# A hybrid decoder layer: the attention loop written in program order, with queries packed on GpSimd

## The chip, the core and the metric

The kernel runs on one core of a Trainium2 chip. The metric is the device time of one launch in microseconds. The core has five engines, each with an instruction stream of its own: TensorE (PE, matmuls and transposes, with its weight loads PEld), VectorE (DVE), ScalarE (ACT), GpSimd (POOL) and SyncE (SP). SP and ACT also issue the DMA requests of this kernel. An engine works through its stream in order; an instruction that must wait for a semaphore holds everything behind it on the same engine. TensorE writes to PSUM banks, which VectorE and ScalarE empty.

## The reference

One layer of a causal decoder trunk on x of 2048 tokens by 1024 channels, float32:

```python
nx = rmsnorm(h, attn_norm_g[l])
proj = jnp.einsum('bsd,dp->bsp', nx, w_in[l])
gq, gk, gv, gr, glow, dq, dk_, dv_ = jnp.split(proj, split_at, axis=-1)
o_a = gla_mixer(gq, gk, gv, glog)                 # 4 heads, chunked gated linear attention
...
o_b = dilated_mixer(dq, dk_, dv_, rel_bias)       # 8 heads of 64, three branches
mixed = jnp.concatenate([o_a, o_b], axis=-1)
h = h + jnp.einsum('bsm,md->bsd', mixed, w_out[l])
nm = rmsnorm(h, mlp_norm_g[l])
a = jnp.square(jax.nn.relu(jnp.einsum('bsd,df->bsf', nm, w_ff1[l])))
h = h + jnp.einsum('bsf,fd->bsd', a, w_ff2[l])
```

The dilated mixer has three branches per head with (window, dilation) pairs (128,1), (512,4) and (2048,16). A branch takes blocks of 128 queries against 256 keys gathered by stride, adds a bias by distance, and does a softmax; the branches are then joined with weights from their softmax denominators.

## The kernel before

The work runs in stages, each of which TensorE should fill. A float32 operand is split in a high and a low part, and a product is three matmuls (L67, L68, L69).

**Input projections (0 to about 589 us).** `groups` (L165 on) are nine ranges of columns of W_in, 256, 264 or 128 wide per half, worked twice (for two halves of the tokens). Each is a product of 2 by 2 blocks done with seven products, so there are 2 x 9 x 7 = 126 jobs. For a job, `load_w` (L181) asks SP for 256 KB parts of the raw weights, `prep` (L187) makes the high and low weights in one of three buffers `combs` (ScalarE L197, VectorE L199), `product` (L270) runs the matmuls, and ScalarE and VectorE add the PSUM banks into `acc` tiles. `finish` (L230) stores results: for the group `dv` two stores per tile, vD and vN (L264, L266), on ScalarE's queue in the second half. `combs` are viewed as (2, 4, 264), so four rows of 256 are 264 elements (1056 bytes) apart whatever the width. `bias_rows` (L320) makes the bias rows, and `spread_bias` (L333) copies them to 128 partitions' worth of rows in DRAM: three DMAs of 1536 KB on SP's queue, after jobs 7 NG + 8, + 14 and + 20 (NG = 9).

**Attention loop (about 589 to 1003 us, L850 to L953).** The dilated mixer is cut in 160 units: per head 4 units for branch 2, 8 for branch 1 and 8 for branch 0; heads go in pairs, and the last pair runs its two branch 0 last. In step k the program writes `scores` of unit k + 3 (AHEAD; L610: matmuls L624 and L626, VectorE's bias and minimum L636, ScalarE's exponential L637), `transpose` of unit k (L643: TensorE L646, copied out as `pt` by ScalarE L653 and VectorE L655 in turn) and `values` of unit k - 2 (LAG; L658: matmuls L665, VectorE's copy L668), taking one instruction of each in turn (`alternate`). Around that:
- `load_head` (L518) brings q and k of a head, in six DMAs, planned 13 units ahead of the head's first unit; `load_v` (L529) and `load_bias` (L547) bring v and the biases.
- `pack_q` (L567) reorders a head's queries for branches 1 and 2, four ScalarE copies of 128x512 per branch (L578), planned from four units ahead.
- `combine` (L684) joins the three branches of a pair once the next pair has begun, in two halves of 8 tiles: a DMA of the stored branches into `cmb` (L692), small VectorE instructions (L699 to L710), and products on GpSimd (L716, L718; on VectorE for the last pair, in four parts of 4 tiles). It writes to mixD by DMAs that are issued some units later.
- `gla_steps` (L798) is the gated linear attention in 16 tiles, one `next` in some steps, from step G0 = 16 on at a rate of GE = 65 in 100 steps; it uses all four compute engines (L783 to L847).
- `load_wo` (L853) brings and splits W_out for the next stage (ScalarE L858, VectorE L859), 8 parts in clumps of 1 to 3 that WOAT ties to four branches of the last two pairs.

The order on each engine here is not the program's: the program is built in a context whose scheduler models the engines' times and reorders instructions by it (`schedule_with_timeline_sim`). Only the first part of the projections is written as a manual schedule. All large tiles come from one pool of 25 slots.

**Out-projection and norms (1003 to 1205 us), MLP (1205 to 2440 us).** The lines from L955 on are not touched.

Of the kernel before, what the change touches and what calls it, by code (L numbers as in the profile page):

```python
# [10 lines left out]
F32 = mybir.dt.float32  # L11
FR = mybir.dt.float32r
# [21 lines left out]
XSC = {0: (3,), 1: (4,), 2: (5,), 3: (), 4: (6,)}  # L34
TOP = (5,)
OTHER = [7, 9, 10, 11, 12] + [14 * k + n for k in (1, 2, 3) for n in (0, 4, 7, 8, 9)]
G0, GE = 16, 65
RELOAD = (10, 11, 12)
BANKS = {"a": 2, "c": 3, "d": 2, "o": 1}

# [1 line left out]
def emit(tc, a, stop=99):  # L42
# [138 lines left out]
    def load_w(g, n, k):  # L181

        if g < 2 * NG:
            _, c0, w = groups[g % NG]
            SP.dma_start(raws[n][:, k, :, :w], w_in[:, 4 * k:4 * k + 4, c0 + n * w:c0 + n * w + w])

    def prep(at):  # L187

        if at >= len(jobs):
            return  # L190
        g, j = jobs[at]
        kind, _, w = groups[g % NG]
        (a11, a12), (a21, a22) = [[raws[n][:, k, :, :w] for k in range(2)] for n in range(2)]
        hi, lo = combs[at % 3][:, 0, :, :w], combs[at % 3][:, 1, :, :w]
# [75 lines left out]
    def product(at, i):  # L270
# [2 lines left out]
        kind, _, w = groups[g % NG]  # L273
        p = ps("acao"[banks[0] % 4])
        banks[0] += 1
        B, W = TB[j], [combs[at % 3][:, q, :, :w] for q in range(2)]
        n = w
        if w == 128:
            n = 512
# [50 lines left out]
            V.tensor_copy(rbo[:, d], p[:8, :384])  # L330
        SP.dma_start(rowD, rbo)

    def spread_bias(d):  # L333

        row = rowD[:, d]
        SP.dma_start(rbD[d].rearrange("h p n -> p h n"),
                     bass.AP(tensor=row.tensor, offset=row.offset, ap=[[0, 128], [3 * 384, 8], [1, 384]]))

    def split(hi, lo, src):
        A.activation(hi, src, AF.Copy)  # L340
# [154 lines left out]
    for at in range(5, len(jobs)):  # L495
        g = jobs[at][0]
        if at + 2 > 6:
            prep(at + 2)
        if at in (7 * NG - 9, 7 * NG - 8):
            back.append(reload(order[at - 7 * NG + 9]))  # L500
        for i in range(4 if groups[g % NG][2] > 128 else 1):
            product(at, i)()
        if g == NG - 1:
            back.pop(0)()
            if at + 2 < 7 * NG:
                back.append(reload(order[at + 2 - 7 * NG + 7]))
# [60 lines left out]
    def pack_q(h, br, part):  # L567
# [10 lines left out]
        A.activation(dst, src.bitcast(F32), AF.Copy)  # L578

    def windows(br, n):  # L580

# [268 lines left out]
    wo = a["w_out"].rearrange("o (c p) n -> p (o c) n", p=128)  # L850
    WO = []

    def load_wo(n):  # L853
        for c in range(len(WO), len(WO) + n):
            raw = slot("woraw")[:, :D]
            w = view(slot("wo", FR), (2, D))
            SP.dma_start(raw, wo[:, c])
            A.activation(w[:, 0], raw, AF.Copy)  # L858
            V.tensor_tensor(w[:, 1], raw, w[:, 0].bitcast(F32), op=OP.subtract)  # L859
            WO.append(w)  # L860
# [16 lines left out]
    def before(b):  # L877
# [4 lines left out]
        if (b.h, b.br) in WOAT:  # L882
            load_wo(WOAT[b.h, b.br])

    def after(b):
        pr, hh = divmod(b.h, 2)
# [11 lines left out]
    for pr in range(4):  # L898
# [3 lines left out]
        for hh, br in seq:  # L902
# [5 lines left out]
                for part in range(4):  # L908
                    at_unit(first - 4 + part if first else 0, pack_q, b.h, br, part)
            if br == 2 and first:  # L910
                at_unit(first - 13, lambda h: pairs.update({h: load_head(h)}), b.h)
                if hh == 0:
                    for half in range(2):
                        c = {}
                        at_unit(first + AHEAD + 1 + 7 * half, lambda c, p, t: c.update(it=combine(p, outs[p, 0], t, 8)),
                                c, pr - 1, 8 * half)
                        for n in (0, 2, 3, 4, 5, 6, 7):
                            at_unit(first + AHEAD + 1 + 7 * half + n, lambda c: next(c["it"], None), c)
            for n in range(0, NT, m):
                units.append(Unit(b, range(n, n + m)))  # L920
    NU = len(units)
    gla = gla_steps()
    for k in range(-AHEAD, NU + LAG):
        tr, pv, sc = iter(()), iter(()), iter(())
        if 0 <= k < NU:
            tr = units[k].transpose()
        if 0 <= k - LAG:
            u = units[k - LAG]
            u.b.v = vs[u.b.h // 2, u.b.br]
            pv = u.values()  # L930
        if k + AHEAD < NU:
            u = units[k + AHEAD]
            if u.ns[0] == 0:
                before(u.b)
            sc = u.scores()
        issue(k)
        for f, *args in plan.get(k + AHEAD, ()):
            f(*args)
        alternate(pv, sc, tr)
        if k >= G0 and (k - G0) * GE // 100 > (k - G0 - 1) * GE // 100:  # L940
            next(gla, None)
        if 0 <= k - LAG:
            u = units[k - LAG]
            if u.b.h == 7 and u.b.br == 0 and u.ns[-1] % 4 == 3 and u.ns[-1] < 15:
                list(combine(3, u.b.O, u.ns[-1] - 3, 4))
            if u.ns[-1] == NT - 1:
                after(u.b)
# [415 lines left out]
```

## Time and profile before

| | us |
|---|---|
| median of 3 runs (2442.3 to 2446.03) | 2444.43 |
| the profiled execution | 2445.35 |
| its span | 2443.6 |
| input projections, about | 0 to 589 |
| attention loop, about | 589 to 1003 |
| out-projection and norms, about | 1003 to 1205 |
| MLP, about | 1205 to 2440 |

In the profile, "busy" is time in which an engine runs compute instructions; register, branch, semaphore and DMA-issuing instructions don't count. SPq and ACTq rows are DMA issues on those engines' queues. A row of the timeline gives start, duration, engine, line, operation, the tile written and the tiles read; in brackets stands how long the engine had been idle and whose end released it. A group row gives the count, the total busy time and the mean of one in ns. Matmuls overlap, so a matmul's duration is longer than the step from one to the next. "Granted clock" is TensorE's clock as a share of full speed. The largest groups of the attention loop are L665 on TensorE (181.1 us in 1200 instructions), L646 (149.6 us in 600), L637 on ScalarE (155.3 us in 384) and L636 on VectorE (126.7 us in 384).

### The profile page before, as it was taken

To read this page: it belongs to the slowest core of one execution; us is meant where nothing else is said; L and a number is where in the kernel's file an instruction comes from. 1 tells how busy PE (TensorE), PEld (TensorE's weight loads), DVE (VectorE), ACT (ScalarE), POOL (GpSimd) and SP (SyncE) were. 2 spreads that over 40 slices of the span, in tenths; PEclk is the share of its full clock that TensorE was granted. 3 is DMA by queue.
4 is the path that set the end of the run, shared out by engine and by line. 5 is a ranking of instruction groups with operands and counts; after the bars stand their busy time and mean duration, and the time that the engine had idled before them with its cause. 6 is when DMAs were issued, how large, how long until landed. Compare 5 with 4: busy or idle time off the path is not lost.

```text
span 2443.6 us, 34989 instructions
## 1 busy us (share of the span) xinstructions
PE 2331.5 (95%) x12648; PEld 1998.8 (82%) x12648; DVE 1585.7 (65%) x2971; ACT 1196.0 (49%) x2215; POOL 488.6 (20%) x425
## 2 busy tenths in 40 slices
PE   6999997999889989999999999999999999999998
PEld 6877887778889888888878887888888888888887
DVE  6877666764567768644677778877774354555554
ACT  5565434534767768323455556655553232234323
POOL 5555435444044534000000000000000000001002
PEclk8999998999999989999999999999999999999999
DMA  6457763747677875567754446644458576556653
GB/s 156 122 157 233 231 197 99 213 147 198 161 186 213 208 197 172 172 215 233 254 195 158 142 147 207 213 168 145 143 194 289 167 276 210 185 189 231 224 165 103
DMA packets 343514, 459.16 MB, mean 188 GB/s; under 512 B 19572, under 2 KB 216453, under 8 KB 337070
## 3 DMA queue, kind: packets, MB, share of 16 engines
q1 hardware_dynamic: 317854, 418.92, 55.8%
q10 hardware_dynamic: 25488, 38.02, 4.4%
q8 instruction: 99, 1.62, 0.3%
q14 instruction: 73, 0.60, 0.1%
HBM read 294.03 MB, written 167.55 MB: 189 GB/s over the span
## 4 chain that ended last, share of the span: by engine, by line
PE 74%; DMA 8%; DVE 7%; ACT 5%; issue 3%; POOL 2%; ACTq 0%; SPq 0%; POOLq 0%; DVEq 0%
PE ps_a L67 8%; PE ps_a L69 8%; PE ps_a L68 8%; PE ps_c L67 7%; PE ps_c L69 7%; PE ps_c L68 7%; PE ps_d L67 4%; PE ps_d L69 4%; PE ps_d L68 4%; PE ps_a L665 3%; PE ps_o L67 3%; PE ps_o L69 3%; PE ps_o L68 3%; PE ps_d L646 2%; DMA wraw<-w_in 2%
## 5 line engine op out<-in xcount | busy, mean ns | idle before, releaser
L1197 POOL TENSOR_TENSOR suma<-suma,gs 128x512 f32<-128x512 f32 x16 | 23.3, 1472 | 1153.2 <-ACT scr L1195 1153.1
L341 DVE TENSOR_TENSOR ca<-ra,ca 128x1024 fp32r<-128x1024 f32 x112 | 137.8, 1230 | 163.1 <-ACT ca L340 163.1
L340 ACT ACTIVATE ca<-ra 128x1024 fp32r<-128x1024 f32 x112 | 118.0, 1053 | 224.9 <-PE ps_c L69 184.5
L340 ACT ACTIVATE w1comb<-w1raw 128x512 fp32r<-128x512 f32 x224 | 139.5, 627 | 159.6 <-PE ps_c L69 56.6
L665 PE MATMUL ps_a<-v,pt 128*128 128x65 f32 x1200 | 181.1, 263 | 13.0 <-ACT pt L653 10.3
L665 PEld LDWEIGHTS ps_a<-v,pt 128*128 128x128 f32 x1200 | 174.5, 199 | 18.6 <-ACT pt L653 12.0
L341 DVE TENSOR_TENSOR w1comb<-w1raw,w1comb 128x512 fp32r<-128x512 f32 x224 | 153.8, 689 | 53.9 <-ACT w1comb L340 53.6
L637 ACT ACTIVATE pe<-pe,O 128x256 f32<-128x256 f32 (+1 forms) x384 | 155.3, 455 | 59.6 <-DVE O L636 54.9
L646 PE MATMUL ps_d<-ident,pe 128*128 128x128 f32 x600 | 149.6, 285 | 8.6 <-DVE gla L796 6.8
L636 DVE CUSTOM_DVE_ANT_0 pe<-ps_c,nb 128x256 f32<-128x256 f32 (+1 forms) x384 | 126.7, 360 | 45.2 <-PE ps_d L646 25.5
L197 ACT ACTIVATE wcomb<-wraw 128x512 fp32r<-128x512 f32 (+2 forms) x126 | 96.4, 774 | 98.7 <-PE ps_a L69 23.3
L199 DVE TENSOR_TENSOR wcomb<-wraw,wcomb 128x512 fp32r<-128x512 f32 (+2 forms) x84 | 99.3, 1187 | 58.7 <-ACT wcomb L197 56.0
L340 ACT ACTIVATE cb<-rb 128x1024 fp32r<-128x1024 f32 x56 | 59.4, 1060 | 159.2 <-PE ps_o L68 105.8
L67 PE MATMUL ps_c<-hb,w1comb 128*128 128x512 f32 x336 | 131.6, 392 | 4.3 <-ACT hb L340 4.3
L68 PE MATMUL ps_c<-hb,w1comb 128*128 128x512 f32 x336 | 131.5, 391 | 1.6 <-DVE w1comb L341 1.6
L69 PE MATMUL ps_c<-hb,w1comb 128*128 128x512 f32 x336 | 131.1, 390 | 0.0
L67 PE MATMUL ps_c<-cb,ca 128*128 128x512 f32 x336 | 130.7, 389 | 0.0
L68 PE MATMUL ps_c<-cb,ca 128*128 128x512 f32 x336 | 130.7, 389 | 0.0
L69 PE MATMUL ps_c<-cb,ca 128*128 128x512 f32 x336 | 130.7, 389 | 0.0
L67 PE MATMUL ps_a<-wcomb,tb 128*128 128x256 f32 (+1 forms) x336 | 99.1, 295 | 19.2 <-ACT acc L297 12.5
L646 PEld LDWEIGHTS ps_d<-ident,pe 128*128 128x128 f32 x600 | 105.5, 184 | 11.1 <-DVE gla L796 7.3
L1063 ACT ACTIVATE acc<-acc 128x512 f32<-128x512 f32 x128 | 79.7, 631 | 56.3 <-DVE acc L1083 35.8
(352 smaller groups left out, 7247.1 us busy)
## 6 DMA issues: line engine op xcount, KB each, us to landing
ra<-actD SPq DMA_DIRECT2D x56, 1024.0 KB, 6.2
actD<-acc SPq DMA_DIRECT2D x192, 256.0 KB, 2.4
rb<-w_ff SPq DMA_DIRECT2D x72, 512.0 KB, 4.6
w1raw<-w_ff SPq DMA_DIRECT2D x32, 1024.0 KB, 5.6
k<-kD SPq DMA_DIRECT2D x32, 512.0 KB, 10.4
rb<-hTD SPq DMA_DIRECT2D x14, 1024.0 KB, 5.6
wraw<-w_in SPq DMA_DIRECT2D x48, 256.0 KB, 3.5
boD<-O SPq DMA_DIRECT2D x8, 1056.0 KB, 5.5
```

Source lines behind the costliest of these rows:

```text
L67: T.matmul(out, sh, mh, start=first, stop=False)
L68: T.matmul(out, sl, mh, start=False, stop=False)
L69: T.matmul(out, sh, ml, start=False, stop=last)
L197: A.activation(hi, src, AF.Copy, scale=sc)
L199: V.tensor_tensor(lo, src, hi.bitcast(F32), op=OP.subtract)
L340: A.activation(hi, src, AF.Copy)
L341: V.tensor_tensor(lo, src, hi.bitcast(F32), op=OP.subtract)
L636: V.tensor_tensor_reduce(p, s, bias, scale=1.0, scalar=BIG, op0=OP.add, op1=OP.min, accum_out=nm)
L637: A.activation(p, p, AF.Exp, bias=nm, scale=-1.0)
L646: T.transpose(pb[:, i * 128:i * 128 + 128], src, ident)
L665: T.matmul(self.b.opsum[:, n % 4], self.pt[:, i * 128:i * 128 + 128], self.b.v[:, blk, cols], start=first, stop=last)
L1063: A.activation(v, v, AF.Relu)
```

## The change

Nothing of the arithmetic changes. In the projections the weight buffers become contiguous for each width (row distance 1 KB for widths 128 and 256; 264 keeps its 1056 bytes), and the three bias DMAs on SP become twelve of 384 KB (two heads each) on ScalarE's queue, after every third job, last branch first. In the attention loop the whole loop is put in a manual schedule for all five engines, so each engine's order is that of the program. `pack_q` copies on GpSimd. `load_head` asks for both copies of q first, 12 units ahead. Biases and v are loaded branch by branch before the loop, and the gated linear attention's first loads come after those of branch 2; its steps begin at k = 8 at a rate of 56 in 100. `combine` of the first three pairs is asked for one unit earlier, its second half after 5 units instead of 7, its first computation three units after the load instead of two. The last pair's four parts ask for their loads ahead, and compute as before where their branch ends. W_out is loaded and split part by part over the last 16 units.

The stream that each engine gets differs as follows. Up to about 350 us and from the out-projection on, order and instructions are the same. TensorE and VectorE have the same instructions as before, ScalarE loses 64 packs and gains 12 DMA issues, GpSimd gains 64 copies. Ten of the twelve bias DMAs come to stand within 16 neighbouring instructions of ScalarE's stream, since that part of the projections is still ordered by the scheduler; among and behind them are stores to vD and vN.

```diff
-G0, GE = 16, 65
+G0, GE = 8, 56
...
-    combs = [view(slot("wcomb", FR), (2, 4, 264)) for _ in range(3)]
+    combs = [slot("wcomb", FR) for _ in range(3)]
...
+    def comb(at, w):
+        t = view(combs[at % 3], (2, 4, max(w, 256)))
+        return [t[:, q, :, :w] for q in range(2)]
...
-    def spread_bias(d):
-        row = rowD[:, d]
-        SP.dma_start(rbD[d].rearrange("h p n -> p h n"),
-                     bass.AP(tensor=row.tensor, offset=row.offset, ap=[[0, 128], [3 * 384, 8], [1, 384]]))
+    def spread_bias(d, h):
+        row = rowD[h:, d]
+        A.dma_start(rbD[d][h:h + 2].rearrange("h p n -> p h n"),
+                    bass.AP(tensor=row.tensor, offset=row.offset, ap=[[0, 128], [3 * 384, 2], [1, 384]]))
...
-        if at in (7 * NG + 8, 7 * NG + 14, 7 * NG + 20):
-            spread_bias((at - 7 * NG - 8) // 6)
+        if 7 * NG + 8 <= at < 7 * NG + 44 and at % 3 == 0:
+            spread_bias(2 - (at - 7 * NG - 8) // 12, (at - 7 * NG - 8) // 3 % 4 * 2)
...
-        for dup in range(2):
-            half = slice(64 * dup, 64 * dup + 64)
+        halves = [slice(64 * dup, 64 * dup + 64) for dup in range(2)]
+        for dup, half in enumerate(halves):
             SP.dma_start(qs[half].bitcast(F32), qD[pr][dup, rows])
-            SP.dma_start(k1[half].bitcast(F32), kD[pr][0, rows])
-            SP.dma_start(k2[half].bitcast(F32), kD[pr][1, rows])
+        for part, t in enumerate((k1, k2)):
+            for half in halves:
+                SP.dma_start(t[half].bitcast(F32), kD[pr][part, rows])
...
-        A.activation(dst, src.bitcast(F32), AF.Copy)
+        G.tensor_copy(dst, src)
...
+    def load_wo(c, raws):
+        raws[c] = slot("woraw")[:, :D]
+        SP.dma_start(raws[c], wo[:, c])
+    def split_wo(c, raws):
+        w = view(slot("wo", FR), (2, D))
+        split(w[:, 0], w[:, 1], raws.pop(c))
+        WO.append(w)
...
-    vs = {(0, br): load_v(0, br) for br in (2, 1, 0)}
+    vs = {}
     for d in (2, 1, 0):
         load_bias(d)
-    gla_start()
-    WOAT = {(7, 2): 3, (7, 1): 2, (6, 0): 2, (7, 0): 1}
+        vs[0, d] = load_v(0, d)
+        if d == 2:
+            gla_start()
...
-                at_unit(first - 13, lambda h: pairs.update({h: load_head(h)}), b.h)
+                at_unit(first - 12, lambda h: pairs.update({h: load_head(h)}), b.h)
                 if hh == 0:
                     for half in range(2):
                         c = {}
-                        at_unit(first + AHEAD + 1 + 7 * half, lambda c, p, t: c.update(it=combine(p, outs[p, 0], t, 8)),
+                        at_unit(first + AHEAD + 5 * half, lambda c, p, t: c.update(it=combine(p, outs[p, 0], t, 8)),
                                 c, pr - 1, 8 * half)
-                        for n in (0, 2, 3, 4, 5, 6, 7):
-                            at_unit(first + AHEAD + 1 + 7 * half + n, lambda c: next(c["it"], None), c)
+                        for n in (0, 3, 4, 5, 6, 7, 8):
+                            at_unit(first + AHEAD + 5 * half + n, lambda c: next(c["it"], None), c)
...
+    for n in range(4):
+        at_unit(NU - 8 + 2 * n + AHEAD, lambda n: (ends.update({n: combine(3, outs[3, 0], 4 * n, 4)}), next(ends[n])), n)
+    for c in range(CH):
+        at_unit(NU - 16 + 2 * c, load_wo, c, raws)
+        at_unit(NU - 12 + 2 * c, split_wo, c, raws)
...
-    for k in range(-AHEAD, NU + LAG):
-        tr, pv, sc = iter(()), iter(()), iter(())
+    with tc.manual_schedule(engines={e.engine for e in (T, V, A, G, SP)}):
+        for k in range(-AHEAD, NU + LAG):
+            tr, pv, sc = iter(()), iter(()), iter(())
...
-            if u.b.h == 7 and u.b.br == 0 and u.ns[-1] % 4 == 3 and u.ns[-1] < 15:
-                list(combine(3, u.b.O, u.ns[-1] - 3, 4))
+                if u.b.h == 7 and u.b.br == 0 and u.ns[-1] % 4 == 3:
+                    list(ends[u.ns[-1] // 4])
...
-    done = outs[3, 0]
-    for _ in gla:
-        pass
-    list(combine(3, done, 12, 4))
-    issue(NU + 99)
+        for _ in gla:
+            pass
+        issue(NU + 99)
```

More of the change, by code (lines that the diff above doesn't have):

```diff
@@ L193, in prep @@
         (a11, a12), (a21, a22) = [[raws[n][:, k, :, :w] for k in range(2)] for n in range(2)]
-        hi, lo = combs[at % 3][:, 0, :, :w], combs[at % 3][:, 1, :, :w]
+        hi, lo = comb(at, w)
         src = {1: a11, 2: a12, 5: a21, 6: a21, 3: a12, 4: a22, 7: a21}[j]
@@ L275, in product @@
         banks[0] += 1
-        B, W = TB[j], [combs[at % 3][:, q, :, :w] for q in range(2)]
+        B, W = TB[j], comb(at, w)
         n = w
@@ L851, in emit @@
     WO = []
[L853 to L860, printed above, removed]
+    def load_wo(c, raws):
[5 more added lines that the diff above has]
+        WO.append(w)
     pairs, outs = {0: load_head(0)}, {}
     ring["pes"], ring["pts"] = view(slot("pe"), (4, 512)), view(slot("pt"), (4, 512))
-    vs = {(0, br): load_v(0, br) for br in (2, 1, 0)}
+    vs = {}
     for d in (2, 1, 0):
         load_bias(d)
-    gla_start()
-    WOAT = {(7, 2): 3, (7, 1): 2, (6, 0): 2, (7, 0): 1}
+        vs[0, d] = load_v(0, d)
+        if d == 2:
+            gla_start()
     def alternate(*streams):
@@ L881, in before @@
         b.head, b.O = pairs[b.h], outs[pr, b.br]
-        if (b.h, b.br) in WOAT:
-            load_wo(WOAT[b.h, b.br])
     def after(b):
@@ L921, in emit @@
     NU = len(units)
-    gla = gla_steps()
-    for k in range(-AHEAD, NU + LAG):
-        tr, pv, sc = iter(()), iter(()), iter(())
[L925 to L943, printed above, removed]
-            if u.b.h == 7 and u.b.br == 0 and u.ns[-1] % 4 == 3 and u.ns[-1] < 15:
-                list(combine(3, u.b.O, u.ns[-1] - 3, 4))
-            if u.ns[-1] == NT - 1:
-                after(u.b)
@@ L948, in emit @@
-    done = outs[3, 0]
-    for _ in gla:
-        pass
-    list(combine(3, done, 12, 4))
-    issue(NU + 99)
+    ends = {}
+    for n in range(4):
+        at_unit(NU - 8 + 2 * n + AHEAD, lambda n: (ends.update({n: combine(3, outs[3, 0], 4 * n, 4)}), next(ends[n])), n)
+    raws = {}
+    for c in range(CH):
+        at_unit(NU - 16 + 2 * c, load_wo, c, raws)
+        at_unit(NU - 12 + 2 * c, split_wo, c, raws)
+    gla = gla_steps()
+    with tc.manual_schedule(engines={e.engine for e in (T, V, A, G, SP)}):
+        for k in range(-AHEAD, NU + LAG):
+            tr, pv, sc = iter(()), iter(()), iter(())
+            if 0 <= k < NU:
+                tr = units[k].transpose()
+            if 0 <= k - LAG:
+                u = units[k - LAG]
+                u.b.v = vs[u.b.h // 2, u.b.br]
+                pv = u.values()
+            if k + AHEAD < NU:
+                u = units[k + AHEAD]
+                if u.ns[0] == 0:
+                    before(u.b)
+                sc = u.scores()
+            issue(k)
+            for f, *args in plan.get(k + AHEAD, ()):
+                f(*args)
+            alternate(pv, sc, tr)
+            if k >= G0 and (k - G0) * GE // 100 > (k - G0 - 1) * GE // 100:
+                next(gla, None)
+            if 0 <= k - LAG:
+                u = units[k - LAG]
+                if u.b.h == 7 and u.b.br == 0 and u.ns[-1] % 4 == 3:
+                    list(ends[u.ns[-1] // 4])
+                if u.ns[-1] == NT - 1:
+                    after(u.b)
+        for _ in gla:
+            pass
+        issue(NU + 99)
```

## The prediction

> **What bounds the kernel now.** I read the page's first, second and fourth parts, then busy time by stage, then PE's waits inside the stage that changes, then the timeline around each large wait.
>
> ```profile
> span 2443.6 us, 34989 instructions
> PE 2331.5 (95%) x12648; PEld 1998.8 (82%) x12648; DVE 1585.7 (65%) x2971; ACT 1196.0 (49%) x2215; POOL 488.6 (20%) x425
> ...
> PE 74%; DMA 8%; DVE 7%; ACT 5%; issue 3%; POOL 2%; ACTq 0%; SPq 0%; POOLq 0%; DVEq 0%
> ```
>
> TensorE is the bound: busy for 95% of the span and 74% of the chain that ended last. So this change can win only where TensorE stands still, where its clock is low, or where its instructions follow one another too slowly. The windows view (start:end, length, then busy microseconds and instructions of PE, PEld, DVE, ACT, POOL, then granted clock, DMA share and GB/s) says where that is:
>
> ```profile
> 346.00:396.00 50.00, 38.61 (x297) 37.62 (x296) 20.60 (x30) 14.44 (x33) 15.35 (x11) 0.86 0.61 180
> ...
> 589.00:1003.00 414.00, 375.02 (x3051) 356.96 (x3052) 289.34 (x1200) 299.88 (x738) 150.62 (x159) 0.95 0.74 194
> ...
> 1205.00:1823.00 618.00, 610.77 (x2688) 504.14 (x2687) 472.95 (x711) 354.83 (x587) 0.54 (x1) 1.00 0.51 172
> ```
>
> The attention loop (589 to 1003 us) leaves TensorE idle for 414.0 - 375.0 = 39.0 us, at a mean clock of 0.95. If the low clock is half speed, it lasted for a tenth of the stage and cost about 0.05 x 414 = 20.7 us. Together 59.7 us are lost there. The MLP, which keeps its order, is full at clock 1.00 and I cost it at nothing. Around 370 us there is one more hole. What the attention loop waits for:
>
> ```profile
> PE ps_a L665 <- ACT pt L653: 10.3, 7, 5.5
> PE ps_d L646 <- DVE gla L796: 6.8, 2, 6.4
> PE ps_c L624 <- DVE O L636: 6.8, 3, 6.3
> PE ps_c L372 <- DMA mx<-mixD: 2.4, 1, 2.4
> ```
>
> Few long waits, not a steady lack: three of 5.5 to 6.4 us make up 18 of the 39 us. And each costs twice, as the clock (the last-but-two column) shows where PE stands or starts again:
>
> ```profile
> 378.00:384.00 6.00, 3.05 (x14) 3.05 (x15) 0.44 (x2) 2.94 (x7) 0.00 (x0) 0.50 0.46 139
> ...
> 590.00:598.00 8.00, 4.77 (x22) 4.50 (x23) 1.53 (x12) 5.35 (x7) 5.94 (x10) 0.57 0.93 276
> ...
> 626.50:632.00 5.50, 5.46 (x31) 5.46 (x31) 1.85 (x7) 2.97 (x7) 0.00 (x0) 0.53 0.95 198
> ...
> 905.00:911.00 6.00, 6.00 (x38) 5.71 (x39) 5.93 (x34) 3.86 (x15) 4.77 (x5) 0.74 0.21 55
> ```
>
> **1. Bias loads in 12 pieces on ScalarE's queue.** Now three 1536 KB requests leave SP's queue together:
>
> ```profile
> 349.79 3.18 SPq L336 DMA_DIRECT2D rbD<-rowD  x3
> ...
> 354.12 19.73 DMA wraw<-w_in
> ...
> 380.50 0.39 ACT L297 ACTIVATE acc<-ps_a 128x264 f32<-128x264 f32 x1 [19.68 <-DMA vD<-acc]
> ...
> 380.95 0.59 PE L67 MATMUL ps_a<-wcomb,tb 128*128 128x264 f32 x1 [11.39 <-ACT acc L297]
> ```
>
> A weight load then takes 19.73 us; ScalarE stands for 19.68 us behind its own stores, and TensorE for 11.39 us until ScalarE empties a PSUM bank. The 378-384 row has its clock at 0.50 after that; reckoned for 5 us, 2.5 us more are lost: a hole of 14 us. The twelve pieces have the same bytes. In the changed program ten of them stand within 16 neighbouring ScalarE instructions, with the vD and vN stores and the next bank's emptying behind them, so the burst is thinned, not gone, and now ScalarE's own queue is held by it. SP loses three issues. Bounds: all 14 us back, or none, because ScalarE is as late as before; a loss beyond that I exclude, since the same bytes pass. I take half, -7 us. The Trainium skill (page "Trainium Kernel Development and Optimization", section "Key Constraints") speaks against a gain: DMAs from SP's, ACT's and POOL's queues share the same 16 engines and interleave, so another queue saves issue time only. By it alone this term would be 0 and the sum 7 us higher; no run here yet shows which.
>
> **2. Weights at multiples of 1 KB.** First and last of 23 matmuls in a row, of a projection product and of the MLP, where operands lie flat:
>
> ```profile
> 537.68 0.39 PE L67 MATMUL ps_a<-tb,wcomb 128*128 128x512 f32 x1
> ...
> 542.79 0.39 PE L68 MATMUL ps_c<-tb,wcomb 128*128 128x512 f32 x1
> ```
> ```profile
> 1399.81 0.39 PE L69 MATMUL ps_a<-hb,w1comb 128*128 128x512 f32 x1
> ...
> 1404.79 0.39 PE L67 MATMUL ps_c<-hb,w1comb 128*128 128x512 f32 x1
> ```
>
> 5.11/22 = 232.3 ns against 4.98/22 = 226.4 ns: 5.9 ns each, and the groups of width 128 have 1008 such matmuls, 5.9 us. For the groups of width 256 (1344 matmuls of 256 columns) no aligned row exists; if they gained the same 5.9 ns it would be 7.9 us more. Bounds 0 (the difference comes from something else, such as the accumulation) and -14; I take -5, nearest the row that exists.
>
> **3. Start of the loop.** Loads by unit and the packs on another engine:
>
> ```profile
> 591.15 1.20 PE L783 MATMUL ps_o<-gla 128*128 128x130 f32 x4 [2.39 <-issue]
> 594.43 0.58 PE L624 MATMUL ps_c<-k,qp 128*128 128x256 f32 x1 [2.08 <-ACT qp L578]
> ```
>
> TensorE stands for 2.39 and 2.08 us, and the 590-598 row gives 0.43 x 8 = 3.4 us of clock: 7.9 us. The first four packs still come after the last projection, one behind the other. Bounds 0 and -7.9; I take half, -4 us.
>
> **4. Packs from ScalarE to GpSimd.**
>
> ```profile
> L578 ACT ACTIVATE qp<-qs 128x512 fp32r<-128x512 f32 x64 | 63.5, 1093 | 4.5 <-DMA qs<-qD 2.3 <-PE ps_a L665 1.9 <-issue 0.3
> ```
> ```profile
> L718 POOL TENSOR_TENSOR O<-O,cmb 128x512 f32<-128x512 f32 x24 | 31.5, 1330 | 0.0
> L716 POOL TENSOR_TENSOR cmb<-cmb,small 128x512 f32<-128x512 f32 x24 | 24.5, 1058 | 0.0
> ...
> L716 POOL TENSOR_TENSOR O<-O,small 128x512 f32<-128x512 f32 x12 | 12.3, 1050 | 12.3 <-DVE small L710 12.1
> L559 POOL COPY nb<-nb 128x256 f32<-128x256 f32 x8 | 4.9, 612 | 2.4 <-DMA nb<-rbD 2.4
> ```
>
> ScalarE gives up 63.5 us. On GpSimd a copy of half the size takes 612 ns, so a pack is about 1.2 us and 64 are 77 us: GpSimd goes from 150.6 to about 228 us of 414. On average that is hidden. But a head has 20 of the 160 units of 414/160 = 2.6 us, 52 us; in the first head of a pair GpSimd must then do both combine halves ((31.5 + 24.5 + 12.3)/6 = 11.4 us each), eight packs (9.6 us) and its share of the gated linear attention ((150.6 - 68.3)/8 = 10 us): 42 of 52 us, in program order. A pack is issued four units, 10.4 us, ahead of its use, about the length of one combine half. So packs can be just late: 0 if they fit; if at each of three pair starts two groups are late by as much as the 6 us above, at twice the cost for the clock, up to +40. I take +4.
>
> **5. The loop in program order, loads placed, combine earlier.** The 59.7 us, less the 7.9 of step 3 and about 4 that stay (the end's wait for mx and its clock), leave 48. The two largest holes:
>
> ```profile
> 617.87 5.86 ACT L578 ACTIVATE qp<-qs 128x512 fp32r<-128x512 f32 x6 [2.31 <-DMA qs<-qD]
> ...
> 626.54 0.69 PE L665 MATMUL ps_a<-v,pt 128*128 128x65 f32 x2 [5.54 <-ACT pt L653]
> ```
> ```profile
> 716.85 6.88 DMA cmb<-boD
> ...
> 724.32 0.58 PE L624 MATMUL ps_c<-k,qs 128*128 128x256 f32 x1 [6.32 <-DVE O L636]
> ```
>
> The first is ScalarE packing six blocks in one go ahead of the pt copy that TensorE needs; with the packs gone from ScalarE it can't recur in that form. The second is VectorE standing in order behind combine's first instruction (L699) for 6.88 us of DMA. In the new plan the load is asked for three units, 7.8 us, ahead of that instruction instead of two, 5.2 us: covered by 0.9 us. What comes late next is the short waits for pt and pe. I take 42 of the 48 as won, -42 us; bounds 0 and -48.
>
> Against it stands the order itself. The changed program takes a values matmul pair, a score and a transpose in turn, where the present one mostly runs the scores of a unit together. Both orders occur now:
>
> ```profile
> 755.46 0.33 PE L665 MATMUL ps_a<-v,pt 128*128 128x65 f32 x2
> 755.60 0.36 PE L626 MATMUL ps_c<-k,qp 128*128 128x256 f32 x1
> 755.80 0.27 PE L646 MATMUL ps_d<-ident,pe 128*128 128x128 f32 x1
> 755.91 0.33 PE L665 MATMUL ps_a<-v,pt 128*128 128x65 f32 x2
> ...
> 758.63 0.28 PE L626 MATMUL ps_c<-k,qp 128*128 128x256 f32 x1
> 758.75 0.33 PE L665 MATMUL ps_a<-v,pt 128*128 128x65 f32 x2
> ...
> 759.03 0.33 PE L665 MATMUL ps_a<-v,pt 128*128 128x65 f32 x2
> ```
>
> In turn: 755.91 - 755.46 = 0.45 us for values, score and transpose. Grouped: 0.28 us for values and transpose and 0.12 us for a score, 0.40 us. A score right behind a values matmul occurs 44 times in the present program and 580 times in the changed one: 536 x 0.047 = +25 us. Bounds 0 (time that a wait would fill anyway) and +27; I take +25, since TensorE is busy for nine tenths of this stage.
>
> The w_out split loses its planned clumps and goes to the last 16 units; VectorE carries it there beside the last combines. It moves work and removes none: 0, bounds -5 and +5. GLA starting eight units earlier: 0, hidden by the same slack.
>
> **The sum.** -7 - 5 - 4 + 4 - 42 + 25 = -29 us. The profiled execution took 2445.35 us (span 2443.6 and 1.75 around it), 0.9 above the median of the runs, 2444.43. From the median: 2415 us.
>
> **The rivals.**
> (a) The interleave costs nothing on the path, because in-order units leave VectorE or ScalarE to set the pace (289 and some 237 us of 414 busy) and TensorE's lost 47 ns fall into waits. For it: TensorE waits in 39 us of the stage already. Against: those waits are clumps. 2415 - 25 = 2390 us.
> (b) Slower: packs late behind combine. GpSimd in strict order is the one engine that gains work, with a pack 10.4 us ahead of its use and 11.4 us of combine in front. It decides where each pack group of the three pair starts and most of the heads waits: the forecast gain of 29 us is gone once new waits and their clock cost 29 + 4 = 33 us, about 5.5 waits of 6 us counted without the clock, or four with 2.5 us of clock each. At the bound of +40 the time is 2415 + 36 = 2451 us. For: its load in those heads is four fifths. Against: pack groups of the other heads meet no combine.
> (c) The change doesn't do what it says in the projections: the bias pieces hold ScalarE as long as before, and the alignment buys nothing. 2415 + 12 = 2427 us, and up to 2439 where steps 3 and 5 too keep a third of their waits. For: the bytes and their place are the same.
> The Trainium skill (page "TensorE: Matmul & The Clock Gate", section "HAM oscillation — how this bites in real kernels") has the clock halve after TensorE gaps above about 3.4 us. The 0.50 behind 11.39 us and 0.53 behind 5.54 us agree; the 0.57 of 590-598, behind gaps of 2.39 and 2.08 us, does not. By the page, late packs of under 3.4 us would cost no clock.
>
> **Chances.** Forecast (2403 to 2427) 0.40; (a) and other cases below 2403, 0.24; (c), 2427 to 2439, 0.12; within 0.2% (4.9 us, about what a measurement can tell from no change) 0.05; (b) and other cases above, 0.19. So faster 0.76, same 0.05, slower 0.19. The range leaves out a tenth on each side: below, (a) with the full bounds of steps 1 to 3 (2390 - 20 = 2370), I take 2374; above, the bound of (b) and a little, 2455. The likeliest case's own range is 2403 to 2427.
>
> **What would show it.** Right: PE idle in attention below 15 us and clock near 1.00 there; no ScalarE wait of 19 us near 370; 128x512 projection matmuls at 226 ns; 0.45 us per values, score and transpose. Wrong: TensorE waiting for qp from GpSimd, or for VectorE behind L699's line; ScalarE waiting on its own DMA issues near 360 us. The prediction fails most if program order makes an engine stand with ready work behind it.

## The result

The changed kernel takes 2480.23 us (median of four runs, 2475.85 to 2485.66). Its ratio to the kernel before is 1.0155, interval 1.0128 to 1.0182: 38 us slower, where 29 us faster was forecast. The profiled execution took 2480.38 us, with a span of 2478.6. In the tables below a ratio r is turned to microseconds as (r - 1) x 2444.

The page of the changed kernel, parts 1 and 4. (Its line numbers are 5 or 6 higher than before in what is quoted here; W_out's split is now done by `split`, L345 on ScalarE and L346 on VectorE.)

```profile
span 2478.6 us, 35025 instructions
PE 2349.6 (95%) x12648; PEld 2022.8 (82%) x12648; DVE 1584.2 (64%) x2971; ACT 1143.0 (46%) x2151; POOL 549.2 (22%) x489
...
PE 72%; DMA 8%; DVE 8%; issue 5%; POOL 3%; ACT 3%; ACTq 0%; SPq 0%; POOLq 0%; DVEq 0%
```

ScalarE has shed 53 us and GpSimd taken on 61, as planned; TensorE has the same 12648 instructions and is 18 us longer at them. The windows view by stage:

```profile
346.00:396.00 50.00, 43.19 (x321) 42.76 (x321) 24.84 (x34) 17.33 (x36) 18.70 (x15) 0.90 0.64 186
...
589.00:1003.00 414.00, 371.66 (x2884) 356.80 (x2884) 262.70 (x1109) 231.32 (x643) 210.27 (x219) 0.93 0.66 177
```

Around 370 us TensorE is busy for 43.2 of 50 us instead of 38.6: that part went as hoped. From 589 to 1003 us it does 2884 matmuls where it did 3051, in about the same busy time, at clock 0.93 instead of 0.95. But that stretch is no longer the whole loop. From the last projection matmul (588.48 us before, 582.12 after) to the first of the out-projection (1002.71 and 1039.08) the loop took 414 us and takes 457, 43 us more; the projections end 6 us earlier, which leaves the loss of some 36 us. The whole loop, before and after:

```profile
588.48:1002.71 414.23, 375.01 (x3054) 356.76 (x3052) 289.25 (x1197) 299.88 (x738) 151.14 (x160) 0.95 0.74 194
```
```profile
582.12:1039.08 456.96, 396.87 (x3046) 380.03 (x3044) 290.66 (x1198) 246.63 (x672) 214.87 (x224) 0.92 0.65 175
```

Of the 43 us, TensorE is busy for 22 (396.9 instead of 375.0) and idle for 21 (60.1 instead of 39.2), so it both works longer at the same matmuls and stands more. Now PE's waits from 580 to 1060 us, and some of the long ones on the timeline:

```profile
PE ps_a L671 <- DVE pt L661: 25.6, 9, 12.3
PE ps_a L671 <- ACT pt L659: 18.4, 7, 6.0
PE ps_c L630 <- POOL qp L584: 6.2, 1, 6.2
```
```profile
588.64 0.58 PE L630 MATMUL ps_c<-k,qp 128*128 128x256 f32 x1 [6.24 <-POOL qp L584]
...
714.94 0.69 PE L671 MATMUL ps_a<-v,pt 128*128 128x65 f32 x2 [4.59 <-ACT pt L659]
...
926.08 0.69 PE L671 MATMUL ps_a<-v,pt 128*128 128x65 f32 x2 [12.29 <-DVE pt L661]
...
1028.66 0.69 PE L671 MATMUL ps_a<-v,pt 128*128 128x65 f32 x2 [5.99 <-ACT pt L659]
```

The old long waits (for the scores' minimum on VectorE behind combine, for GLA) have gone, and others of the same size and larger have come: 44 of the 60 us are values matmuls that wait for `pt`, TensorE's own transposes copied out by VectorE or ScalarE. The copy itself takes some 0.6 us; the runs below show for two of the waits what stands ahead of it on its engine.

Three theories follow: (A) program order costs, by TensorE taking turns and by engines held behind one late instruction; (B) GpSimd's packs cost; (C) the new times of the loads cost.

### The profile page after: what moved, and what is told of

Same layout as the page of the kernel before. It is cut to its first block, busy times and chain, and to the rows that moved or that the text cites. A ratio compares the mean times of both kernels' runs of the same rounds, so it can differ in the third digit from the quotient of the medians.

```text
span 2478.6 us, 35025 instructions
## 1 busy us (share of the span) xinstructions
PE 2349.6 (95%) x12648; PEld 2022.8 (82%) x12648; DVE 1584.2 (64%) x2971; ACT 1143.0 (46%) x2151; POOL 549.2 (22%) x489
## 4 chain that ended last, share of the span: by engine, by line
PE 72%; DMA 8%; DVE 8%; issue 5%; POOL 3%; ACT 3%; ACTq 0%; SPq 0%; POOLq 0%; DVEq 0%
PE ps_a L67 8%; PE ps_a L68 8%; PE ps_a L69 8%; PE ps_c L67 6%; PE ps_c L69 6%; PE ps_c L68 6%; PE ps_d L68 4%; PE ps_d L69 4%; PE ps_d L67 4%; PE ps_o L67 3%; PE ps_o L68 3%; PE ps_o L69 3%; PE ps_a L671 3%; PE ps_d L652 2%; PE ps_c L632 2%
## 5 line engine op out<-in xcount | busy, mean ns | idle before, releaser
L671 PE MATMUL ps_a<-v,pt 128*128 128x65 f32 x1200 | 212.9, 262 | 44.1 <-DVE pt L661 25.6
L346 DVE TENSOR_TENSOR ca<-ra,ca 128x1024 fp32r<-128x1024 f32 x112 | 137.6, 1230 | 158.5 <-ACT ca L345 158.5
L671 PEld LDWEIGHTS ps_a<-v,pt 128*128 128x128 f32 x1200 | 193.6, 202 | 51.9 <-DVE pt L661 27.9
L345 ACT ACTIVATE ca<-ra 128x1024 fp32r<-128x1024 f32 x112 | 117.9, 1053 | 215.7 <-PE ps_c L69 173.3
L345 ACT ACTIVATE w1comb<-w1raw 128x512 fp32r<-128x512 f32 x224 | 139.6, 627 | 157.5 <-PE ps_c L69 56.6
L346 DVE TENSOR_TENSOR w1comb<-w1raw,w1comb 128x512 fp32r<-128x512 f32 x224 | 153.7, 689 | 55.4 <-ACT w1comb L345 55.2
L652 PE MATMUL ps_d<-ident,pe 128*128 128x128 f32 x600 | 168.7, 284 | 2.4 <-DVE stats L93 1.0
L345 ACT ACTIVATE cb<-rb 128x1024 fp32r<-128x1024 f32 x56 | 59.4, 1061 | 170.0 <-PE ps_o L68 94.1
L94 POOL TENSOR_TENSOR stats<-stats,mhalf 128x1 f32<-128x1 f32 (+1 forms) x64 | 46.1, 725 | 405.2 <-DVE stats L93 341.9
L346 DVE TENSOR_TENSOR cb<-rb,cb 128x1024 fp32r<-128x1024 f32 x56 | 68.2, 1222 | 58.8 <-ACT cb L345 58.8
```

Of the source, the lines that this page charges most:

```text
L652: T.transpose(pb[:, i * 128:i * 128 + 128], src, ident)
L671: T.matmul(self.b.opsum[:, n % 4], self.pt[:, i * 128:i * 128 + 128], self.b.v[:, blk, cols], start=first, stop=last)
```

## The experiments

Each was run on the chip beside the kernel before; all but two have an interval.

### One step of the order at a time: scores together

```diff
-            alternate(pv, sc, tr)
+            alternate(pv, tr)
+            alternate(sc)
```

> The changed kernel, but in each step the scores of a unit are written together, behind the values and transposes, instead of in turn with them. Nothing else differs. If a score behind a values matmul costs 0.045 to 0.05 us of TensorE time and that time lies on the path (536 more of them than before), the time falls by about 25 us, to some 2455 us. If the loss comes from waits (engines held in program order) and TensorE's extra time falls into them, it falls by less than 8 us.

Measured: 2459.15 us, ratio 1.0076 [1.0053, 1.0099]. Against the changed kernel that is 0.0079, 19 us. A score right behind a values matmul is now found 24 times instead of 580. The edit also moves VectorE's and ScalarE's part of the scores behind the pt copies, so it isn't TensorE's order alone that changes. But the windows row of its loop shows whose time went:

```profile
580.55:1013.76 433.21, 369.38 (x3045) 353.89 (x3044) 296.42 (x1198) 245.07 (x672) 215.60 (x224) 0.91 0.68 185
```

TensorE is busy for 369.4 us instead of 396.9 in the same matmuls, and idle for 63.8 instead of 60.1: it is the busy time that fell. The turn-taking is real and on the path; it is half of the slowdown and not all.

### The whole manual schedule

```diff
-    with tc.manual_schedule(engines={e.engine for e in (T, V, A, G, SP)}):
+    if True:
```

> The changed kernel with the manual schedule of the attention loop taken away: the scheduler orders the loop as it did before, all other edits stay (packs on GpSimd, load placement, combine times, bias pieces, aligned weights). If the order of the instructions is what costs, the time comes to 2435 us or less (the loss of 37 us goes, and the 6 us won in the projections stay). If packs on GpSimd or the new load and combine times cost, it stays above 2465 us.

Measured: 2418.3 us, ratio 0.9909 [0.9887, 0.993]: faster than before by 22 us and than the changed kernel by 60. All other edits together are a gain; with the loop in program order the same edits are a loss. Its windows row of the loop:

```profile
589.00:1003.00 414.00, 392.17 (x3164) 372.75 (x3165) 313.15 (x1247) 248.71 (x679) 212.48 (x223) 0.97 0.74 197
```

In the same 414 us TensorE now does 3164 matmuls, 280 more than in the changed kernel, and idles 22 us. The loop itself is over at 973.81 us: it takes 391 us, where it took 414 and, in program order, 457.

### SyncE's queue

```diff
-    with tc.manual_schedule(engines={e.engine for e in (T, V, A, G, SP)}):
+    with tc.manual_schedule(engines={e.engine for e in (T, V, A, G)}):
```

> The changed kernel with SyncE left out of the manual schedule, so that only the order of DMA requests on SP's queue is the scheduler's again. If SP's program order makes combine's loads late (the wait of 12.3 us behind a cmb load of 17.3 us, and its clock), the time falls by 12 to 25 us, to 2455 to 2468 us. If those loads are late for another reason (traffic), it stays within 6 us of 2480.

Measured: 2479.5 us, ratio 1.0159 [1.0137, 1.0181]: no change. That doesn't clear the place of the requests, because the scheduler put the ones that matter in the same place, head 7's q and k right ahead of combine's load:

```profile
895.53 1.92 SPq L529 DMA_DIRECT2D qs<-qD  x2
897.50 2.56 SPq L532 DMA_DIRECT2D k<-kD  x4
900.16 8.13 SPq L698 DMA_DIRECT2D cmb<-boD  x2
```

The two parts of that load took 16.8 and 17.8 us to land, as in program order. The run shows only that the scheduler's order on SP is no better here; the place of one load is tried below.

### The packs, in both orders

```diff
-        G.tensor_copy(dst, src)
+        A.activation(dst, src.bitcast(F32), AF.Copy)
```

> The changed kernel with the 64 packs on ScalarE again, in the same program order. If packs on GpSimd cost (a wait of 6.2 us at the start, VectorE's small combine instructions of 1 to 2 us instead of 0.2 to 0.4 us beside them, v loads late behind GpSimd's queue), the time falls by 10 to 20 us. If ScalarE's 63.5 us of packs ahead of the pt copies were the dearer place, it rises by 5 to 25 us.

> The changed kernel in the scheduler's order with the packs on ScalarE again. If packs on GpSimd are part of why that order with the other edits gives 2418 us, the time rises by 8 us or more, to 2426 or above (packs on ScalarE cost 8 us in program order). If the gain is from the placed loads, the bias pieces and the weights, it stays within 5 us of 2418.

Measured: in program order 2488.09 us, ratio 1.019 [1.0166, 1.0215], against 1.0155; in the scheduler's order 2436.82 us, ratio 0.9958 [0.9942, 0.9974], against 0.9909. The intervals overlap in program order, where it is about 9 us, and don't in the scheduler's, where it is 12. So packs on GpSimd win time in the order in which it can be told; theory B falls, as far as it says that they cost on balance. The first expected direction (packs on GpSimd cost 10 to 20 us) was a miss.

### TensorE's order alone, put into the kernel before

```diff
-    for k in range(-AHEAD, NU + LAG):
...
+    with tc.manual_schedule(engines={e.engine for e in (T,)}):
+        for k in range(-AHEAD, NU + LAG):
...
```

> The kernel before with TensorE alone in program order inside the attention loop (580 scores right behind a values matmul instead of 44); VectorE, ScalarE, GpSimd and SyncE are still ordered by the scheduler, and nothing else of the change is made. If the turn-taking costs 0.04 us each on the path, as the 21 us of the run with scores together say, the time rises by 15 to 25 us, to 2460 to 2470 us. If it costs only together with the other engines' order, it stays within 6 us of 2443.

Measured: 2481.87 us, ratio 1.0145 [1.0123, 1.0167]: 35 us, more than expected. A loss of the size of the changed kernel's can be had from this one line, in a kernel without the other edits. Only part of it is the turn-taking: in the loop TensorE is busy for 388.1 us instead of 375.0 and idle for 53.9 instead of 39.2. Its waits of at least 0.9 us from 580 to 1060 us add up to 52 us against 32 before. That TensorE, held to its own order, waits with other work ready is the likely reason; it wasn't taken apart.

### Head 7's load

The wait of 12.29 us at 926 follows from a load. The chain of waits of the changed kernel, VectorE's wait for that load, and SP's queue just before:

```profile
904.46 17.32 DMA cmb<-boD
...
925.42 0.61 DVE pt L661
```
```profile
919.98 0.17 DVE L705 TENSOR_TENSOR small<-O,cmb 128x16 f32<-128x16 f32 x1 [9.21 <-DMA cmb<-boD]
```
```profile
897.74 2.25 SPq L529 DMA_DIRECT2D qs<-qD  x2
900.03 3.31 SPq L532 DMA_DIRECT2D k<-kD  x4
904.03 8.46 SPq L698 DMA_DIRECT2D cmb<-boD  x2
```

In the last pair both heads' branches 2 and 1 come first, so head 7 begins 12 units after head 6, and "12 units ahead" falls on the start of head 6: 3 MB are asked for just in front of combine's load, which then takes 17.3 us; the load that the prediction went by took 6.9. VectorE stands behind it at combine's first instruction (L705, L699 in the kernel before), and the pt copy behind VectorE.

```diff
-                at_unit(first - 12, lambda h: pairs.update({h: load_head(h)}), b.h)
+                at_unit(first - (8 if b.h == 7 else 12), lambda h: pairs.update({h: load_head(h)}), b.h)
```

> The changed kernel with scores together and one load moved: head 7's q and k (3 MB) are asked for 8 units ahead of its first unit instead of 12, so behind combine's first load of the last pair start and not three units ahead of it. If those 3 MB make that load take 17 us, the wait of 15 us (there at 903 us) goes with its clock: 2459 falls by 12 to 20 us, to 2439 to 2447. If the load is late for another reason, it stays within 4 us of 2459.

Measured, on top of scores together: 2453.0 us, ratio 1.0024 [1.0011, 1.0038], against 1.0076: 13 us, at the low end of what was expected. Combine's load now lands in 4.2 to 6.0 us, and VectorE waits 1.1 us for it at L705; in the run with scores together it waits 12.5. TensorE's wait shrank and didn't go; the timeline's row of scores together and that of this run:

```profile
903.17 0.69 PE L671 MATMUL ps_a<-v,pt 128*128 128x65 f32 x2 [15.15 <-DVE pt L661]
```
```profile
898.52 0.69 PE L671 MATMUL ps_a<-v,pt 128*128 128x65 f32 x2 [4.17 <-DVE pt L661]
```

### The last units: combine's products, or W_out's splits

```diff
-        X = V if pr == 3 else G
+        X = G
```

> As the run with head 7's load later, and the products of the last pair's combines on GpSimd instead of VectorE (16 and 4 instructions of 0.69 us leave VectorE's stream). If the waits of TensorE in the last 16 units (some 17 us behind VectorE) come from combine standing in one piece in VectorE's order, the time falls by a further 5 to 12 us. If W_out's splits are what holds VectorE, or GpSimd's slower products come late, it changes by less than 4 us or rises.

Measured: 2459.08 us, ratio 1.0054 [1.0035, 1.0073]: some 7 us slower than the run with head 7's load later, with intervals that just touch. The hoped-for gain was a miss: either combine's products are not what holds VectorE there, or GpSimd's come as late. The timeline of the run with head 7's load later shows something else that holds it:

```profile
966.07 0.31 ACT L826 ACTIVATE gla<-gla 128x128 f32<-128x128 f32 x1
966.37 1.04 ACT L345 ACTIVATE wo<-woraw 128x1024 fp32r<-128x1024 f32 x1
967.50 1.23 DVE L346 TENSOR_TENSOR wo<-woraw,wo 128x1024 fp32r<-128x1024 f32 x1 [4.50 <-issue]
968.98 0.68 DVE L661 COPY pt<-ps_d 128x512 f32<-128x512 f32 x1
969.72 0.69 PE L671 MATMUL ps_a<-v,pt 128*128 128x65 f32 x2 [4.17 <-DVE pt L661]
```

ScalarE does a block of GLA, then W_out's high part; VectorE's low part (L346) is next in VectorE's order and waits 4.5 us for it, though the pt copy behind it could have gone, since the last transpose that it copies ended at 965.08 us; TensorE waits 4.17 us for that copy. Taking the two parts apart by one unit:

```diff
...
-        at_unit(NU - 12 + 2 * c, split_wo, c, raws)
+        at_unit(NU - 13 + 2 * c, high_wo, c, raws)
+        at_unit(NU - 12 + 2 * c, low_wo, c, raws)
```

> As the run with scores together and head 7's load later, and each split of W_out in two steps: ScalarE's high part one unit ahead of VectorE's low part, instead of both at the same place. If VectorE stands (4.5 us at 963 us) because its low part is written ahead of the pt copy and waits for ScalarE, whose high part is behind a GLA block in its own order, three of the waits in the last units (4.2, 2.1 and 2.1 us) shrink: the time falls by 6 to 14 us against that run. If the last units wait for VectorE's own work or for loads, it stays within 3 us.

Measured: 2442.91 us, ratio 0.9996 [0.9984, 1.0008], against 1.0024: 7 us won, within the expectation. With three edits of the order the changed kernel is back at the time of before, but not at the 0.9909 of the scheduler's order.

### Which engine's order holds the rest

Base: the scheduler's order with head 7's load later.

> The changed kernel in the scheduler's order with head 7's load 8 units ahead instead of 12. Its longest attention wait behind a cmb load (4.2 us, the load 9.0 us) should shrink as it did in program order: 3 to 8 us less than 2418. If the scheduler places that load by itself, it stays within 3 us.

Measured: 2413.65 us, ratio 0.987 [0.9854, 0.9887], 32 us faster than before: the version that beats both kernels. Against 0.9909 the gain is some 10 us by the ratios and 5 by the times (3 to 8 were expected), with intervals that touch. On this base one group of engines at a time was put in program order (TensorE with scores together, the others as in the change):

> Scheduler's order with head 7's load later (2413.7 us), but TensorE alone in program order with scores together. If the 31 us that are left in the mended program order come from TensorE's fixed order (it meets a transpose or values whose input is late with ready scores behind), the time rises by 15 to 30 us, to 2429 to 2444. If they come from the order on VectorE and ScalarE, it stays within 6 us of 2414.

> Scheduler's order with head 7's load later, but VectorE and ScalarE alone in program order, TensorE, GpSimd and SyncE by the scheduler. If VectorE's and ScalarE's fixed order holds the rest (combine's and W_out's instructions ahead of pt copies that TensorE needs), the time rises by 15 to 30 us, to 2429 to 2444. If TensorE's order does, it stays within 6 us of 2414.

> Scheduler's order with head 7's load later, VectorE alone in program order. If VectorE's order holds most of the 50 us (its values copies wait for TensorE 70 us in all, with score work ready behind them), the time rises by 30 us or more, to 2444 or above. If ScalarE's does, it stays below 2429.

> Scheduler's order with head 7's load later, ScalarE alone in program order. If ScalarE's order holds most of the 50 us, the time rises by 30 us or more, to 2444 or above; if VectorE's does, it stays below 2429. If both stay below 2429, it is the two together.

| in program order | time, us | ratio to before | interval |
|---|---|---|---|
| none | 2413.65 | 0.987 | 0.9854 to 0.9887 |
| TensorE, scores together | 2412.64 | 0.9887 | 0.9862 to 0.9912 |
| ScalarE | 2425.95 | 0.9923 | 0.9892 to 0.9953 |
| VectorE | 2435.95 | 0.9965 | 0.995 to 0.998 |
| VectorE and ScalarE | 2463.93 | 1.0091 | 1.0064 to 1.0117 |

TensorE's order costs nothing measurable once the scores run together. VectorE's costs 23 us, ScalarE's 13, both together 54, more than the sum and more than the 15 to 30 that were expected; VectorE's 2435.95 fell between its two expected cases. GpSimd's order was not tried by itself. The loop with none fixed, and with VectorE and ScalarE fixed:

```profile
583.80:973.01 389.21, 366.73 (x3054) 351.95 (x3052) 294.95 (x1196) 245.30 (x673) 214.37 (x224) 0.97 0.77 206
```
```profile
581.74:1022.34 440.60, 391.81 (x3045) 370.70 (x3044) 288.39 (x1198) 243.24 (x673) 212.56 (x224) 0.90 0.68 180
```

Of 51 us more, TensorE is idle for 26 and busy for 25, at a clock of 0.90 instead of 0.97, though its own order was the scheduler's. That the two are dearer together because each makes the other late, with ready work behind, is a reading and wasn't shown. What VectorE waits for, in the loop, with VectorE and ScalarE fixed, and with TensorE fixed:

```profile
DVE O L674 <- PE ps_a L671: 70.3, 43, 6.1
DVE gla L802 <- PE ps_d L801: 20.1, 8, 7.8
```
```profile
DVE O L674 <- PE ps_a L671: 31.9, 40, 2.3
...
DVE gla L802 <- PE ps_d L801: 4.3, 2, 2.5
```

With its order fixed, VectorE stands 70 us ahead of the values copies instead of 32, and 20 us ahead of GLA's masks instead of 4 (28 and 7 with none fixed). These are VectorE's waits; what they cost on the path is not read from them.

### The projections

> The kernel before with the weight buffers contiguous for each width, nothing else. Read from the steps of the trace, not from the time: 128x512 projection matmuls 228 ns apart instead of 232.5 (as in the changed kernel), so 4 us over 1008 of them; the hole of 11.4 us at 381 us stays. If the shorter step comes from something else in the change, it stays at 232.5 ns.

> The kernel before with the bias copies in twelve pieces on ScalarE's queue, nothing else. If the pieces are what shortened the hole near 370 us, TensorE's longest wait there falls from 11.4 us to about 3 to 5 us, and the last projection matmul comes 4 to 7 us earlier than 588.5 us. If they only move the wait, it stays within 2 us.

Both are the kernel before with one edit, executed once each, so they are read by single steps and waits and not by the time. Aligned weights: first and last of 24 matmuls in a row,

```profile
537.75 0.39 PE L67 MATMUL ps_a<-tb,wcomb 128*128 128x512 f32 x1
...
542.97 0.39 PE L69 MATMUL ps_a<-tb,wcomb 128*128 128x512 f32 x1
```

are 5.22/23 = 227 ns apart (over 820 such steps 228.1 against 232.5). But the steps of the 256-column matmuls, where the weights are not the stationary operand as in those of 512 columns but the moving one, go from 118.3 to 119.9 ns. The last projection matmul comes at 587.09 us instead of 588.48. These 1.4 us can't be told from chance: in the run with TensorE's order put into the kernel before, whose projections are not changed, it comes at 589.89. Bias pieces: it comes at 582.09 us, 6.4 us earlier, with these waits in place of the one of 11.39 us:

```profile
367.55 0.58 PE L67 MATMUL ps_o<-wcomb,tb 128*128 128x256 f32 x1 [5.28 <-ACT acc L310]
...
378.79 0.39 PE L67 MATMUL ps_c<-wcomb,tb 128*128 128x264 f32 x1 [2.35 <-ACT wcomb L197]
```

The fourteen runs that have both edits come at 580.6 to 585.2 us, no earlier than this one. ScalarE still stands behind its own DMAs, for 10.9 and 9.1 us in two pieces where it was 19.7 in one. Whether the smaller pieces or the other queue did this was not taken apart.

## Why the prediction was wrong, step by step

- **Step 1, bias pieces, -7 us: right in size.** -6.4 us. The -7 was half of a hole, taken between all and none; the burst is thinned, as the step said, but ScalarE stands as long as before (one of the step's reasons for no gain) and only TensorE's wait is shorter. The rule of the Trainium skill quoted there (another queue saves issue time only) would have given 0; since pieces and queue changed together, no run here shows it wrong.
- **Step 2, aligned weights, -5 us: right in mechanism, too large.** The 128x512 matmuls gained 4.4 ns of the 5.9 expected; the 256-column ones, costed from no gain to a gain, lost 1.6 ns each. Over 1008 and 1344 matmuls that leaves an estimated -4.4 + 2.2 = -2.2 us, too little to be seen in the end of the projections.
- **Step 3, start of the loop, -4 us: wrong.** TensorE's first score came 6.24 us behind the last projection matmul, for GpSimd's first pack; before it was 594.43 - 588.76 = 5.7 us, with GLA matmuls in between. In the first 12 us from 588 (before) and 582 us the clock was 0.72 in both. Nothing was won.
- **Step 4, packs, +4 us: wrong sign.** A pack took 1107 ns on GpSimd (1.2 us was the estimate). The combine halves in front didn't make packs late: TensorE waits for a pack once in the loop, at its start. The packs won 12 us in the scheduler's order and some 9, not clear of the intervals, in program order; ScalarE's relief is the likely reason.
- **Step 5, the waits, -42 us: this is the step that failed.** It took the old waits as gone and "the short waits for pt and pe" as what comes late next. It traced each old wait to its cause and not one instruction of the new order to its. It reckoned 59.7 us lost in the loop, 39 idle and 20.7 by the clock, and 42 of them won; reckoned in the same way the changed loop loses 97, 60 idle and 0.08 x 457 = 37 by the clock. What came next were waits of 4 to 12 us, because engines held in program order stand behind an instruction that is not ready: VectorE behind W_out's low part (7 us by its run) and behind combine's load, which the plan itself had put behind 3 MB (13 us). That wait, VectorE behind L699's line, was one of the prediction's own signs of being wrong. VectorE's waits ahead of values copies and GLA grow too, but no run shows what these cost. The lead of "three units, 7.8 us" was set against a load of 6.88 us without looking at what else is asked for just ahead of it.
- **The turn-taking, +25 us: nearly right.** 19 us of the time by the run with scores together, and 27.5 us of TensorE's busy time.
- **Rivals.** Slower was given 19%, by GpSimd's packs late behind combine, at 2451 us. The kernel is slower by more, and by another mechanism; rival (b) is refuted by the pack runs and by the one wait for a pack. The mechanism named last in the prediction, "program order makes an engine stand with ready work behind it", had been given neither a price nor a chance of its own.

The account from the runs, from the kernel before: all edits but the order -22 us; TensorE's turns +19; head 7's load +13; W_out's split +7; the rest of the order 0.9996 - 0.9909 = 0.0087, +21: sum +38, as measured. The sum closes by construction, since each term is the step from one run to the next; in another order of the steps the terms would differ. Beside the scheduler's order with head 7's load later, at 0.987, 31 us are left instead of 21. By the last runs the rest sits in VectorE's and ScalarE's order, GpSimd's being untried; which of their instructions carry it wasn't taken apart further.

## What to carry to other kernels

A hand-written order must be judged by its own heads of queue: for each engine, ask of the instruction that is written first in a step whether it is ready, and what ready work stands behind it; work off the path (a weight split, a combine) belongs behind the copies that TensorE waits for. A load's lead counts only with the bytes that are asked for ahead of it. And when an order and other edits change together, run the edits in the old order first: here they were a gain of 22 us, and 32 with one load moved, that the new order hid.

## What the runs showed of the hardware that was not expected

VectorE's smallest instructions can take as long as GpSimd's large ones. Two of combine's 128x16 operations in the changed kernel, first in a half with no GpSimd instruction beside it, then beside GpSimd's products, and GpSimd's products of that moment:

```profile
692.66 0.17 DVE L706 TENSOR_TENSOR small<-small,cmb 128x16 f32<-128x16 f32 x1
692.87 0.18 DVE L708 TENSOR_TENSOR small<-small,O 128x16 f32<-128x16 f32 x1
```
```profile
708.66 0.96 DVE L706 TENSOR_TENSOR small<-small,cmb 128x16 f32<-128x16 f32 x1
709.73 1.25 DVE L708 TENSOR_TENSOR small<-small,O 128x16 f32<-128x16 f32 x1
```
```profile
708.55 1.04 POOL L722 TENSOR_TENSOR cmb<-cmb,small 128x512 f32<-128x512 f32 x1
709.68 1.27 POOL L724 TENSOR_TENSOR O<-O,cmb 128x512 f32<-128x512 f32 x1
```

0.96 and 1.25 us against 0.17 and 0.18, and each of the long ones ends about 0.03 us behind a product of GpSimd. Not every one beside GpSimd is held: at 820.03 us L706 took 0.17 us, with a product from 820.04 on. The Trainium skill (page "GPSIMD Engine Reference", section "Specifications") has GpSimd share its SBUF interfaces with VectorE, with contention for VectorE instructions of two SBUF inputs; the trace agrees. Which share of the wait of 4.59 us at 714.94 this makes was not tried by itself.
